# Moving the mixers' weight loads from the SyncE queue to the GpSimd queue

## The chip, the cores and the metric

The kernel runs on one core of one Trainium2 chip. The metric is the device time of one execution in microseconds (us); 1770.11 us is the median of three runs of the kernel before. Engines are named as in the profile: PE is TensorE (matmuls), PEld its weight loads, DVE VectorE, ACT ScalarE, POOL GpSimd, SP SyncE. SP computes nothing; it issues DMAs one after the other, each after its own waits.

## What is computed

Two layers over 256 latent and 256 context tokens of width 1024. Each layer has a mixer (three kinds of attention side by side, gated and merged) and a channel mixer (a dense SwiGLU in layer 0, a top-2 mixture of eight SwiGLU experts in layer 1). Cut to the mixer, which the change is about:

```python
h = modulate(rms_norm(x, norm_mix[i]), sh1, sc1)            # sh1, sc1, g1 ... from c @ w_ada[i]
p_kv, p_q, p_gate = split_last(h @ w_in[i], ...)
y_na  = neighbourhood_attention(q_na, k_na, v_na, k_na_c, v_na_c, rpb[i], n_rows)   # 4 heads
y_gqa = blocked_attention(q_g, k_g, v_g, k_g_c, v_g_c, GQA_SCALE)                   # 8 heads, 2 kv heads
y_mla = blocked_attention(q_m, k_m, v_m, k_m_c, v_m_c, MLA_SCALE)                   # 4 heads
x = x + g1 * merge_branches(y_na, y_gqa, y_mla, p_gate, w_o_na, w_o_gqa, w_o_mla, w_out)
# in layer 0 the context stream goes through the same mixer
```

## The kernel before

All weights are float32 in HBM and are used as pairs of float16 (a high and a low part). A weight tile of up to 128 x 2048 floats (1 MB) is loaded by `load_raw` (L302) into one of four buffers called raw. `split_w` then makes the pair: ACT writes wh (L269), DVE writes wl (L266, from raw and wh). Three such pairs exist (WB = 3). PE multiplies with them (L332 to L334: wh by the high part, wh by the low part, wl by the high part). A raw buffer is free again when the wl of its tile is written; a pair is free when PE has used it. `load_raw` also fetches the adaLN weights of layer 0 (in_ada): those raw tiles are read by PE itself (L426, `ada0_sums`), two tiles for each of twelve sums, four sums in `start` and eight among the jobs of the mixer of layer 0. `load_raw` issues every one of these transfers on SP.

The stages follow one another: `start` (norm, the first four adaLN sums, the first two weight tiles ckv_kg and kna; it has eight further raw buffers), the mixer of layer 0 (about 45 to 440 us), `ffn` (to about 790 us), the mixer of layer 1 (to about 1045 us), then routing and the experts (in_wm, the rest).

In a mixer, PE computes scores of a pair of heads (L936), ACT and DVE make the softmax (L913, L269 and L266 into pn, three buffers), and SP issues a DMA transpose of each pn into pt (L920, three buffers, 4 in a unit of work, 96 in all); PE multiplies pt by the values (L952). `weave` puts the units among the dense work of the mixer. What a buffer's next user must wait for is put in by the framework, and a planner in it lays out each engine's order when the program is built; the order is not simply that of the text. SP's order holds weight loads, loads of the position bias (`head_bias`, L743), rope tables (L386) and the transposes, each behind the one before it. POOL has seven memsets in the whole program, one of them in each mixer (krp, L756).

The functions that name the queue of a load:

Of the kernel before, what the change touches and what calls it, by code (L numbers as in the profile page):

```python
# [249 lines left out]
def trunk(tc, A, out):  # L250
    nc = tc.nc
# [3 lines left out]
    def nm(p="t"):  # L255
        cnt[0] += 1
        return f"{p}{cnt[0]}"
# [10 lines left out]
    def split(hi, lo, src, scale):  # L268
        h = S.activation(hi, src, AF.Copy, scale=scale)  # L269
        return h, stt(lo, src, scale, hi, OP.mult, OP.subtract)  # L270
# [10 lines left out]
    def dram(name, off, w):  # L281
        src = A[name]
        return bass.AP(tensor=src.tensor, offset=src.offset + off, ap=[[w, 128], [1, w]])
# [14 lines left out]
    def new_raw():  # L298
        pool, tag, n = take("raw", raw_slots)
        return pool.tile([128, 2048], FT, tag=tag, bufs=n, name=nm("raw"))  # L300

    def load_raw(name, off, w=2048):  # L302
        raw = new_raw()
        nc.sync.dma_start(raw[:, :w], dram(name, off, w))
        return raw

    def load_w(name, off, w=2048):
        return split_w(load_raw(name, off, w), w)

    def new_parts():  # L310
        pool, tag, n = take("wb", wb_slots)
        return [pool.tile([128, 2048], F16, tag=tag + h, bufs=n, name=nm("w" + h)) for h in "hl"]
# [9 lines left out]
    def split_w(raw, w, parts=None, step=1024):  # L322
        if parts is None:
            parts = new_parts()
        hi, lo = parts
        for a in range(0, w, step):
            b = min(w, a + step)
            issued[0] = split(hi[:, a:b], lo[:, a:b], raw[:, a:b], WS)
        return hi, lo
# [58 lines left out]
    def ada_tile(pool, cb, t):  # L388

        raw = load_raw("ada1", t * 128 * 2048)  # L390
        for j in range(2):
            ch = 2 * t + j
            for s in range(2):
                if s == 1 and ch >= 16:
                    continue
                scr = pool.tile([128, D], F16, tag="scr", bufs=1, name=nm("scr"))
                stt(scr, raw[:, j * D:(j + 1) * D], 0.5, cb[:, s, :], OP.mult, OP.mult,
                    accum_out=mod[1][:, ch, s:s + 1])

    def ada_group(i, g):  # L400

        s = slice(8 * g, 8 * g + 8)
        b = cv(f"b{i}")[:, s]
        n = 1 if (i == 1 and g >= 2) else 2
        m = mod[i][:, s, :n]
        if i == 1:
            add(m, m, b[:, :, None].to_broadcast([128, 8, n]))
        half, what = divmod(g, 3)
        if what == 0:
            V.tensor_scalar(sm[:, i, half, :, :n], m, AS, None, op0=OP.mult)  # L410
        elif what == 1:
            nrm = cv(("nm" if half == 0 else "nf") + str(i))
            u = am[:, i, half, :, :n]
            V.tensor_scalar(u, m, 1.0, AS, op0=OP.add, op1=OP.mult)
            mul(u, u, nrm[:, :, None].to_broadcast([128, 8, n]))
        else:
            V.tensor_scalar(m, m, US, None, op0=OP.mult)

    def ada0_sums(c):


        ps = pg()
        for s in range(2):
            w = load_raw("ada0", (2 * c + s) * 128 * 2048)
            for k in range(4):
                T.matmul(ps[32 * k:32 * k + 32], c32[:, 4 * s + k, :], w[:, 512 * k:512 * k + 512],  # L426
                         start=(s == 0), stop=(s == 1))
        row = st.tile([128, 512], FT, tag="sq", bufs=3, name=nm("row"))
        S.copy(row, ps)
        return row  # L430

    def ada0_cols(row, ch):

        pm = pb([128, 4, 2])
        for k in range(4):
            T.matmul(pm[:, k], row[:, 128 * k:128 * k + 128], cm("pick"), start=True, stop=True)
        m = mod[0][:, ch:ch + 4, :]
        add(m, pm, cv("b0")[:, ch:ch + 4, None].to_broadcast([128, 4, 2]))
        return m
# [12 lines left out]
    def ada0_jobs():  # L452
        q = []
        for c in range(4, 12):
            q.append(lambda c=c: ada0_cols(ada0_sums(c), 4 * c))
            if c % 2:
                q.append(lambda g=c // 2: ada_group(0, g))
        return q

    def ada1_jobs(pool):  # L460
        cb = pool.tile([128, 2, D], FT, name="cb")
        cbf = cb.rearrange("p a b -> p (a b)")

        def prep():
            nc.sync.dma_start(cbf, bass.AP(tensor=A["cc"].tensor, offset=A["cc"].offset, ap=[[0, 128], [1, 2 * D]]))
            t = new_raw()
            S.activation(t, cbf, AF.Tanh, scale=0.5)
            stt(cbf, t, 1.0, cbf, OP.add, OP.mult)

        q = [prep]  # L470
        for t in range(24):
            q.append(lambda t=t: ada_tile(pool, cb, t))
            if t % 4 == 3:
                q.append(lambda g=t // 4: ada_group(1, g))
        return q
# [102 lines left out]
    def start(pool, nrm):  # L578

        raw_slots.append((pool, "raw2", 8))  # L580
        offs, _ = offsets(stream_names(0))
        nrm.alloc()
        for k in range(KD):
            nrm.square(0, k)
        wa = load_w("ws0", offs["ckv_kg"])
        nrm.sums(0)
        first_mod(0)
        wb = load_w("ws0", offs["kna"])
        nrm.spread(0)
        nrm.apply(0, range(0, 4))  # L590
        p4 = [pa() for _ in range(4)]
        jobs = [(p4[0], wa, 0, ALL), (p4[1], wa, 1, ALL), (p4[2], wb, 0, ALL), (p4[3], wb, 1, ALL)]
        first_mod(1)
        group(nrm, jobs, range(0, 4))
        nrm.apply(0, range(4, 8))
        group(nrm, jobs, range(4, 8))
        raw_slots.pop()
        return p4

    def mixer(pool, i, ada_q, nrm, nxt, first=None):  # L600
# [13 lines left out]
        def W(name, n=0):  # L614
            r = load_w(f"ws{i}", offs[name], tile_width(name))
            ada(n)
            return r
# [423 lines left out]
        for j in range(2):  # L1041
            w = W(f"wout{j}")
            for a in range(2):
                out_chunk(w, 2 * j + a, qs)
        w = [W("wout2"), W("wout3")]
        if last:
            presplit.append(split_w(load_raw("wm", 0), 2048, step=2048))
        for p, c in enumerate(halves):
            for d in range(4, 8):
# [64 lines left out]
    with tc.tile_pool(name="s0", bufs=1, reuse_waits="tile") as pool:  # L1114
        p4_0 = start(pool, n_m0)
    with tc.tile_pool(name="m0", bufs=1, reuse_waits="tile") as pool:
        mixer(pool, 0, ada0_jobs(), n_m0, n_f0, p4_0)
    with tc.tile_pool(name="f0", bufs=1, reuse_waits="tile") as pool:
        ffn(pool, ada1_jobs(pool), n_f0, n_m1)
    px = tc.alloc_tile_pool(name="px", bufs=1, reuse_waits="tile")  # L1120
# [8 lines left out]
    ones16 = px.tile([128, 128], F16, name="ones16")  # L1129
    V.memset(ones16, 1.0)  # L1130
    with tc.tile_pool(name="m1", bufs=1, reuse_waits="tile") as pool:
        mixer(pool, 1, [], n_m1, n_f1)


# [322 lines left out]
```

## Time and profile before

| | before |
|---|---|
| time, median of 3 runs (range) | 1770.11 us (1768.71 to 1772.60) |
| the profiled execution, its time | 1770.29 us |
| its span, first to last instruction | 1768.3 us |
| PE, DVE, ACT, POOL busy | 93%, 76%, 59%, 0% |
| granted TensorE clock, mean | 0.976 |
| DMA transposes, weight loads in mixers and start | 96; 68 of in_ws and 24 of in_ada |

The profiled execution lies 0.18 us above the median of the runs, and 2.0 us of its time lie outside its span. The stages differ in their limit, so the views are read stage by stage: the table of stretches gives the busy time of each engine in a window, the waits say what ended the idle time before an instruction, the timeline lists instructions in order of time, and the DMA issues give the time from the issue of a transfer to its landing.

### The profile page before, as it was taken

Reading aid. Unit: us, or ns where it says so; the run is one execution under the profiler, and the core shown is the slowest. Engines: PE = TensorE matmul, PEld = TensorE weight load, DVE = VectorE, ACT = ScalarE, POOL = GpSimd, SP = SyncE. Lnnn points to the kernel's source line nnn. Section 1 sums busy time; section 2 is a strip of 40 time slices with the busy share of each in tenths; the row PEclk is TensorE's granted clock in tenths of the full one; section 3 lists DMA queues with packets and bytes.
Section 4 is the critical chain, followed back from the end, with each engine's and each line's share of the span. In section 5 each row is a group of like instructions: output and inputs, shape, how many; then the busy total and the mean of one; then the engine's idle time right before and its main releaser. Section 6 shows DMA issues by size and latency. Waiting matters only on the chain. (4 is left out here: it accounts for less than half of the span.)

```text
span 1768.3 us, 37807 instructions
## 1 busy us (share of the span) xinstructions
PE 1644.8 (93%) x16157; PEld 1085.5 (61%) x16157; DVE 1351.6 (76%) x1908; ACT 1038.1 (59%) x1354; POOL 1.3 (0%) x7
## 2 busy tenths in 40 slices
PE   5999899999999999999878998999999989999996
PEld 2554335446644444467656877787868686868683
DVE  4577657455886554547787778999999999999996
ACT  3456546343422332224666558888877888878784
POOL 0000000000000000000000000000000000000000
PEclk9999899999999999999998998999999999999998
DMA  9263388452465445534536687999999999999990
GB/s 390 102 155 93 104 257 220 135 193 96 143 219 209 167 161 172 192 111 138 161 79 145 185 306 315 424 413 423 420 415 385 422 418 420 422 400 400 403 384 26
DMA packets 149920, 451.93 MB, mean 256 GB/s; under 512 B 92144, under 2 KB 95344, under 8 KB 103024
## 3 DMA queue, kind: packets, MB, share of 16 engines
q1 hardware_dynamic: 148768, 448.50, 69.0%
q8 instruction: 128, 2.10, 0.5%
q10 hardware_dynamic: 976, 0.94, 0.2%
q14 instruction: 48, 0.39, 0.1%
HBM read 427.38 MB, written 1.05 MB: 242 GB/s over the span
## 5 line engine op out<-in xcount | busy, mean ns | idle before, releaser
L266 DVE SCALAR_TENSOR_TENSOR wl<-raw,wh 128x2048 f16<-128x2048 f32 (+1 forms) x476 | 818.3, 1739 | 54.0 <-ACT wh L269 50.5
L269 ACT ACTIVATE wh<-raw 128x2048 f16<-128x2048 f32 (+1 forms) x474 | 684.3, 1464 | 269.8 <-PE pa L333 94.0
L334 PEld LDWEIGHTS <-wl 128*128 128x128 f16 x4346 | 427.2, 98 | 175.1 <-DVE wl L266 53.3
L332 PEld LDWEIGHTS <-wh 128*128 128x128 f16 x4346 | 428.6, 99 | 129.0 <-issue 17.7
L333 PEld LDWEIGHTS <-wh 128*128 128x128 f16 x4346 | 427.7, 98 | 115.2 <-issue 7.9
L334 PE MATMUL pa<-xg,wl 128*128 128x96 f16 x2816 | 374.6, 207 | 36.2 <-DVE wl L266 35.6
L333 PE MATMUL pa<-xg,wh 128*128 128x96 f16 x2816 | 373.5, 206 | 0.2 <-ACT xg L1254 0.2
L332 PE MATMUL pa<-xg,wh 128*128 128x96 f16 x2816 | 373.4, 206 | 0.0
L332 PE MATMUL pg<-hh,wh 128*128 128x512 f16 (+1 forms) x512 | 170.2, 333 | 5.0 <-ACT gt L972 2.1
L332 PE MATMUL pa<-hh,wh 128*128 128x512 f16 (+1 forms) x480 | 167.5, 355 | 6.1 <-ACT hh L552 6.1
L333 PE MATMUL pa<-hl,wh 128*128 128x512 f16 (+1 forms) x480 | 169.2, 354 | 1.7 <-DVE hl L266 1.7
L334 PE MATMUL pg<-hh,wl 128*128 128x512 f16 (+1 forms) x512 | 169.6, 332 | 0.7 <-DVE wl L266 0.7
L333 PE MATMUL pg<-hl,wh 128*128 128x512 f16 (+1 forms) x512 | 170.0, 332 | 0.0
L334 PE MATMUL pa<-hh,wl 128*128 128x512 f16 (+1 forms) x480 | 169.1, 353 | 0.0
L266 DVE SCALAR_TENSOR_TENSOR scr<-raw,cb 128x1024 f16<-128x1024 f32 x64 | 78.4, 1225 | 78.9 <-DMA raw<-in_ada 77.8
L1317 PE MATMUL pg<-wl,hdh 128*96 128x512 f16 x352 | 133.4, 379 | 0.5 <-DVE wl L266 0.2
L1318 PE MATMUL pg<-wh,hdl 128*96 128x512 f16 x352 | 133.4, 379 | 0.0
L1316 PE MATMUL pg<-wh,hdh 128*96 128x512 f16 x352 | 132.3, 379 | 0.0
L266 DVE SCALAR_TENSOR_TENSOR pn<-P,sml,pn 128x512 f16<-128x512 f32 (+1 forms) x96 | 60.9, 660 | 32.7 <-ACT pn L269 32.2
L269 ACT ACTIVATE pn<-P,sml 128x512 f16<-128x512 f32 (+1 forms) x96 | 59.1, 648 | 38.3 <-DMA pt<-pn 33.3
L913 ACT ACTIVATE P<-pa,sml 128x512 f32<-128x512 f32 (+1 forms) x96 | 58.0, 611 | 32.3 <-DVE sml L911 22.8
L333 PE MATMUL pg<-dl,wh 128*128 128x512 f16 (+1 forms) x198 | 70.4, 355 | 0.0
(250 smaller groups left out, 1860.6 us busy)
## 6 DMA issues: line engine op xcount, KB each, us to landing
raw<-in_wm SPq DMA_DIRECT2D x264, 1024.0 KB, 8.2
raw<-in_ws SPq DMA_DIRECT2D x52, 1024.0 KB, 4.8
raw<-in_ada SPq DMA_DIRECT2D x48, 1024.0 KB, 5.1
raw<-in_ws SPq DMA_DIRECT2D x18, 768.0 KB, 4.9
raw<-in_ws SPq DMA_DIRECT2D x16, 704.0 KB, 4.1
raw<-in_ws SPq DMA_DIRECT2D x16, 640.0 KB, 4.0
raw<-in_ws SPq DMA_DIRECT2D x4, 832.0 KB, 11.6
xT<-in_xt SPq DMA_DIRECT2D x4, 512.0 KB, 6.3
```

Source lines behind the costliest of these rows:

```text
L266: return V.scalar_tensor_tensor(o, a, s, b, op0=op0, op1=op1, **kw)
L269: h = S.activation(hi, src, AF.Copy, scale=scale)
L332: T.matmul(ps, sh, mh, start=first, stop=False)
L333: T.matmul(ps, sh, ml, start=False, stop=False)
L334: T.matmul(ps, sl, mh, start=False, stop=last)
L913: S.activation(P[t], ps[t], AF.Exp, bias=nb[:, t:t + 1], scale=sc, accum_out=sums[:, t:t + 1])
L1316: T.matmul(py, hdh[:, f], w[0][:, c], start=begin, stop=False)
L1317: T.matmul(py, hdh[:, f], w[1][:, c], start=False, stop=False)
L1318: T.matmul(py, hdl[:, f], w[0][:, c], start=False, stop=end)
```

## The change

`load_raw` issues on `queue[0]` instead of on `nc.sync`. This is `nc.gpsimd` while the two mixers are traced and `nc.sync` elsewhere; inside the last mixer it goes back to `nc.sync` just before the first load of the experts' weights. So 82 loads go to POOL: 32 of in_ws and 16 of in_ada in layer 0, where `start` keeps its two and eight on SP, and 34 of in_ws in layer 1. The loads of the bias and the rope tables and the transposes stay on SP. Number and size of the buffers, and all computing, stay.

```diff
+    queue = [nc.sync]
+
     def load_raw(name, off, w=2048):
         raw = new_raw()
-        nc.sync.dma_start(raw[:, :w], dram(name, off, w))
+        queue[0].dma_start(raw[:, :w], dram(name, off, w))
         return raw
...
         if last:
+            queue[0] = nc.sync
             presplit.append(split_w(load_raw("wm", 0), 2048, step=2048))
...
+        queue[0] = nc.gpsimd
         mixer(pool, 0, ada0_jobs(), n_m0, n_f0, p4_0)
+        queue[0] = nc.sync
...
+        queue[0] = nc.gpsimd
         mixer(pool, 1, [], n_m1, n_f1)
```

## Rows read from the trace of the kernel before

**Rows 1.** The page: busy time of the engines; all DMA packets by size.

```profile
PE 1644.8 (93%) x16157; PEld 1085.5 (61%) x16157; DVE 1351.6 (76%) x1908; ACT 1038.1 (59%) x1354; POOL 1.3 (0%) x7
...
DMA packets 149920, 451.93 MB, mean 256 GB/s; under 512 B 92144, under 2 KB 95344, under 8 KB 103024
```

**Rows 2.** Stretches: us; PE, PEld, DVE, ACT, POOL busy; clock; DMA share, GB/s.

```profile
100.00:212.00 112.00, 102.87 (x606) 51.02 (x606) 85.70 (x214) 69.77 (x157) 0.00 (x0) 0.94 0.40 99
212.00:260.00 48.00, 43.64 (x299) 20.33 (x295) 24.97 (x58) 22.58 (x50) 0.00 (x0) 1.00 0.84 267
260.00:345.00 85.00, 84.98 (x487) 40.69 (x480) 51.94 (x102) 42.46 (x87) 0.00 (x0) 1.00 0.67 180
...
900.00:960.00 60.00, 45.55 (x328) 29.80 (x328) 49.67 (x106) 37.59 (x81) 0.00 (x0) 0.86 0.57 132
```

**Rows 3.** Waits, whole span: who waited for whom; us in total, times, longest.

```profile
ACT pn L269 <- DMA pt<-pn: 33.3, 20, 5.5
...
PE pa L936 <- ACT P L913: 8.8, 5, 2.8
PE pb L952 <- DMA pt<-pn: 8.5, 6, 2.7
```

**Rows 4.** Tile pt, 212 to 300 us: transposes' issue (ns) and landing, min/median/max.

```profile
L920 SPq DMA_TRANSPOSE pt<-pn x22: 1194/1238/3943, 220.1 to 289.4; - x22
...
DMA to landing us min/median/max: 2.3/3.9/6.8
```

**Rows 5.** Tile pt, 857 to 987 us: landing of the 32 transposes.

```profile
DMA to landing us min/median/max: 3.1/3.4/4.9
```

**Rows 6.** Timeline from 209 us: start, duration, engine, line, what, count, idle before.

```profile
211.27 2.76 PE L426 MATMUL pg<-raw,c 128*32 128x512 f32 x18
...
212.40 0.34 SPq L304 DMA_DIRECT2D raw<-in_ws  x1
...
214.95 1.92 PE L426 MATMUL pg<-raw,c 128*32 128x512 f32 x14
...
217.40 2.01 ACT L269 ACTIVATE wh<-raw 128x1024 f16<-128x1024 f32 x2
...
220.07 2.51 SPq L920 DMA_TRANSPOSE pt<-pn  x2
...
222.28 0.39 PE L334 MATMUL pg<-hh,wl 128*128 128x512 f16 x1 [0.72 <-DVE wl L266]
...
222.63 1.05 SPq L304 DMA_DIRECT2D raw<-in_ada  x2
```

**Rows 7.** DMA issues, 212.35 to 212.90 us: KB, us to landing.

```profile
raw<-in_ws SPq DMA_DIRECT2D x1, 1024.0 KB, 4.9
```

**Rows 8.** Timeline of SP, start of the program.

```profile
8.50 6.46 SPq L304 DMA_DIRECT2D raw<-in_ada  x4
...
20.83 53.52 SPq L304 DMA_DIRECT2D raw<-in_ws  x8
```

**Rows 9.** DMA issues at 8.50 us (first of four) and at 14.62 us (last).

```profile
raw<-in_ada SPq DMA_DIRECT2D x1, 1024.0 KB, 18.3
...
raw<-in_ada SPq DMA_DIRECT2D x1, 1024.0 KB, 19.6
```

**Rows 10.** Timeline of PE: its use of the first and of the last of these four.

```profile
30.90 1.94 PE L426 MATMUL pg<-raw,c 128*32 128x512 f32 x8
...
42.33 1.06 PE L426 MATMUL pg<-raw,c 128*32 128x512 f32 x8
```

**Rows 11.** Timeline of ACT, layer 0's third branch: it waits for a weight tile.

```profile
360.44 1.36 ACT L269 ACTIVATE wh<-raw 128x1024 f16<-128x1024 f32 x2 [2.20 <-DMA raw<-in_ws]
```

**Rows 12.** Timelines of SP and ACT: a late load of layer 1's mixer, its split.

```profile
1019.79 0.33 SPq L304 DMA_DIRECT2D raw<-in_ws  x1
...
1029.84 1.06 ACT L269 ACTIVATE wh<-raw 128x1024 f16<-128x1024 f32 x1 [0.21 <-PE pg L333]
```

**Rows 13.** Tile krp: POOL's longest instructions, ns min/median/max.

```profile
L756 POOL MEMSET krp<- x2: 417/420/422, 1.0 to 382.7; 128x384 f32 x2
```

## Prediction

> **What bounds the kernel now.** I read the page first: PE is busy for 93% of the span, POOL for nothing [rows 1]. The change touches the start and the two mixers alone, so the table of stretches is next. From 260 to 345 us PE is busy for 84.98 of 85 us [rows 2]: nothing on a queue can be won there. It has 9.1 us of idle time from 100 to 212 us, 4.4 from 212 to 260 and 14.5 from 900 to 960 (112 - 102.87, 48 - 43.64, 60 - 45.55) [rows 2]. These 28 us hold nearly all that a better queue could give back, and 900 to 960 has a granted clock of 0.86, so a little more than the idle time hangs on them. The waits say what ended such idle time: PE waited for transposed probabilities (pt) for 8.5 us in six places, and for ACT's exponential for 8.8 us in five; ACT in turn waited 33.3 us, in 20 places, for a transpose to finish reading a pn buffer [rows 3]. None of the three lines names a weight load. So a queue change can win by quicker transposes, hardly by earlier weights.
>
> **What the change removes.** 82 loads leave SP, at 0.34 us of issue each [rows 6], 28 us of SP time; SP bounds nothing, so this counts only where a load and a transpose hold each other up.
>
> *Loads held behind transposes.* At 216.87 us (214.95 + 1.92) PE has read a raw tile of in_ada, which frees its buffer; the next load into the freed buffers is issued at 222.63, because SP stood at the transposes of 220.07, themselves waiting [rows 6]. So loads here come some 6 us late, and on POOL they would not. Worth to the end: about 0, because from 260 us on PE is full [rows 2] and no wait of [rows 3] is for a raw tile. In layer 1 the load of 1019.79 has some 5 us to spare: landed 4.9 us later [rows 7], 1024.7, it is split at 1029.84 when PE frees the pair [rows 12].
>
> *Transposes held behind loads.* The issue of a transpose takes 1238 ns at the median and up to 3943 where loads fill the queue (212 to 300 us), and it lands after 2.3 to 6.8 us [rows 4]; in layer 1 after 3.1 to 4.9, median 3.4 [rows 5]. If the median came down to the minimum, that were 1.6 us (3.9 - 2.3) for 22 transposes and 0.3 us for 32. But the bytes of the loads are still moved, beside the transposes instead of ahead of them. Ends: -8.5 us (every wait of PE for pt goes) and +7 (below). I take -0.5, near nothing: the landing of 3.1 us in layer 1 is the best of 32, so even alone in the queue a transpose leaves PE most of its wait.
>
> [...]
>
> **What the change adds.** *POOL's own price.* No row shows a DMA issued by POOL. Nearest below: SP's load issue, 0.34 us [rows 6], and POOL's longest instruction, 0.42 us [rows 13]; nearest above: an issue of SP that writes many descriptors, 1.24 us at the median, 3.94 at worst [rows 4]. Against the 0.34 us of now a load so lands between 0.3 us earlier (a queue without others ahead; no row excludes it) and 3.6 us later (3.94 - 0.34). I take 0.9 later (1.24 - 0.34), the ordinary issue that writes many descriptors. [...]
>
> Where does later hurt? Where the buffer, not the queue, held the load, and the use follows at once. The load of 212.40 follows the reading of the tile in its buffer at once (L426 from 211.27), lands 4.9 us later at 217.30, ACT splits it at 217.40, and PE sits 0.72 us at 222.28 until wl is there [rows 6, 7]. This one is on the path: +0.9 us (ends -0.3, +3.6). The tile that ACT awaited 2.20 us at 360.44 [rows 11] is like it on ACT, but PE, full through 345 us and fed from three pairs, has work ahead of it: 0, with +1.8 (twice 0.9) if that cover is gone. In layer 1 the 5 us to spare cover all.
>
> *What queues behind POOL's waits.* A POOL load waits for its raw buffer; behind it stand only later loads, which need later buffers, and the krp memset (0.42 us [rows 13]), awaited long after. Cost 0.
>
> *The start.* Here one queue has an order that is worth something. SP has issued four loads of in_ada from 8.50 to 14.62 us when the mixer's first loads come at 20.83 [rows 8]; these four land 18.3 and 19.6 us after their issue, at 26.8 and 34.2, one each 2.47 us, so the DMA engines have a backlog of 13 us at 20.83 [rows 9]. Now the mixer's first four loads (1 + 0.81 + 0.81 + 1 MB) queue behind it. On POOL they run beside it: 3.62 x 2.47 = 8.9 us of transfers. PE reads the first in_ada tile at 30.90, 4.1 us after it landed, and the last at 42.33, 8.1 us after [rows 9, 10]. With equal shares from 21.2 (20.83 + 0.34) the first lands at 21.2 + 2 x 5.6 = 32.4, 1.5 us after PE wants it, and the last at 34.2 + 8.9 = 43.1, 0.8 after. PE runs its instructions in their order and is full afterwards, so this stays: +1.5 us. Ends: 0 (the older backlog goes first, as now) and +4.8 (the new loads go first, 8.9 - 4.1).
>
> **Sum.** +1.5 (start) + 0.9 (load of 212.40) - 0.5 (transposes) + 0 = +1.9 us on the profiled execution's 1770.29 (1768.3 of span and 2.0 outside it): 1772.2, and as the median of the runs is 0.18 lower, 1772.0 us, 0.1% above before. A measurement of this kernel tells about 0.2% (3.5 us) from no change, so faster means below 1766.6 and slower above 1773.7. The single ends add up to 1770.1 + 0 - 0.3 - 8.5 = 1761.3 and, without the +7 that is a rival's, 1770.1 + 4.8 + 3.6 + 1.8 = 1780.3.
>
> The planner lays out the engines' orders anew, with loads it no longer has to fit between transposes. What that moves, no row tells; the idle time it can fill is the 28 us above. I count it in the chances.
>
> **Rivals.**
> 1. *Faster: the transposes decide.* With short issues always, ACT's waits for pn shorten, and PE's 8.5 us for pt and the part of the 8.8 us behind ACT go. For it: the issues of 3.94 us [rows 4], PE's 14.5 idle us beside transposes [rows 2, 3]. Against: from 100 to 212 us loads are few (99 GB/s) and PE is idle for 9.1 us all the same [rows 2]. With all 8.5 and nothing lost, 1770.1 - 8.5 = 1761.6; with the start's 1.5 lost, 1763.
> 2. *Slower: POOL is slow to write a load's descriptors.* If a load lands 3.6 us later, the one at 212.40 costs 3.6 and, where the cover at 360 us is thinner than I think, two further ones 1.8 together, and the start 1.5 to 4.8: 1770.1 + 3.6 + 1.8 + 3 = 1778.5. It decides from some 1.5 us of extra time on. For it: the backlog and the lack of slack in [rows 6, 9, 11]; against: layer 1, with 5 us to spare. [...]
> 3. *Slower: packets alternate.* A transpose is some 960 packets (92144 under 512 B for 96), a load 128 [rows 1]. If the engines take turns between queues packet by packet, every transpose beside a load waits out that load, 2.5 us, also one issued after it. ACT's 11 waits in the two stretches with loads would grow by 27 us, of which PE, at 8.5 for 33.3 [rows 3], sees 7: 1779.
> 4. *Nothing happens,* because loads wait for buffers and not for the queue, as in layer 1: 1770. It lies within the forecast's own case.
>
> **Chances.** Forecast with rival 4, 42%: its own range 1768 to 1775, 36 points within 0.2%, 6 slower. Rival 1, 22%: 20 faster, 2 same. Rival 2, 24%: 22 slower, 2 same. Rival 3, 12%: 10 slower, 2 same. So faster 0.20, same 0.42, slower 0.38. The range of 8 in 10 takes in most of rivals 1 to 3: 1761 to 1781.
>
> **What would show it.** In the trace of the changed kernel: SP holds transposes, bias and rope alone in the mixers, and the issue of a transpose no longer exceeds 2 us from 212 to 300 us. PE's readings of in_ada tiles at the start come 1 to 2 us later and the first PE idle time there names a DMA. The load of g0_3 (the one of 212.40) lands some 6 us after its buffer is free, not 5. The transposes of layer 1 still land after 3 us or more, and PE from 900 to 960 us is still idle for some 14 us. Wrong, if that idle time falls by 5 us or more (rival 1), if raw tiles appear among the waits of ACT and PE in the mixers with more than a few us (rival 2), or if transposes land after 6 us and more beside loads (rival 3).

## The result and the profile after

The changed kernel takes 1798.03 us (median of 4 runs, 1797.66 to 1801.09) beside 1770.42 of the kernel before on the same chip: ratio 1.0155, 95% interval 1.014 to 1.017. It is 27.6 us slower; the prediction was 1772.0 with a range of 1761 to 1781. The profiled execution of after took 1801.09 us, the longest of the four; its span is 1799.2.

The page of after: busy time of the engines, and the new queue of POOL (packets, MB, share of the 16 DMA engines). [Rows 1] has the same line of before.

```profile
PE 1652.8 (92%) x16157; PEld 1089.2 (61%) x16157; DVE 1350.9 (75%) x1908; ACT 1038.5 (58%) x1354; POOL 44.8 (2%) x89
...
q0 software_dynamic: 11808, 74.19, 12.1%
```

PE is busy 8.0 us longer with the same 16157 matmuls, the span is 30.9 us longer: 22.9 us are new idle time of PE, 8.0 are matmuls at a lower clock (0.967 granted on the mean, 0.976 in before). To see where, I cut both traces at the same pieces of work: from the first transpose to the FFN's first activation (mixer of layer 0), to the first transpose of layer 1 (FFN), and to the first load of in_wm (mixer of layer 1). Stretches of before (start:end, length, PE, PEld, DVE, ACT, POOL busy, clock, DMA share, GB/s):

```profile
95.20:471.90 376.70, 359.49 (x2175) 188.23 (x2174) 238.69 (x517) 182.35 (x370) 0.42 (x1) 0.97 0.53 155
471.90:857.90 386.00, 381.97 (x2020) 197.09 (x2018) 232.61 (x390) 125.81 (x190) 0.00 (x0) 1.00 0.48 167
857.90:1026.80 168.90, 146.03 (x1206) 112.64 (x1205) 134.01 (x293) 102.80 (x208) 0.00 (x0) 0.92 0.62 156
```

The same three of after:

```profile
95.90:497.10 401.20, 364.50 (x2175) 190.26 (x2174) 238.19 (x517) 182.17 (x370) 20.08 (x38) 0.95 0.51 146
497.10:882.50 385.40, 381.75 (x2020) 197.13 (x2018) 232.56 (x390) 126.00 (x190) 6.78 (x13) 1.00 0.48 167
882.50:1057.70 175.20, 148.68 (x1205) 114.30 (x1204) 133.58 (x293) 102.93 (x208) 11.64 (x22) 0.88 0.59 150
```

Layer 0's mixer is 24.5 us longer (401.2 - 376.7): 19.5 of idle time (36.7 against 17.2) and 5.0 of slower matmuls. Layer 1's is 6.3 us longer, 3.6 and 2.7. The start is 0.7 longer, the FFN 0.6 shorter, the experts unchanged (741.5 in both). Of the three waits shown in [rows 3] the first and the last grew, and one that was 1.6 us in before (longest 0.7) now stands behind them with 22.2 (waits of after: who for whom, us, times, longest):

```profile
ACT pn L269 <- DMA pt<-pn: 41.6, 20, 5.1
...
PE pb L954 <- DMA pt<-pn: 24.4, 8, 10.3
...
ACT qg L269 <- PE pb L954: 22.2, 7, 9.9
```

PE's wait for transposes went from 8.5 to 24.4 us, the longest one from 2.7 to 10.3. The transposes from 212 to 300 us, to be held beside [rows 4] (issue in ns, then landing in us, min/median/max each):

```profile
L922 SPq DMA_TRANSPOSE pt<-pn x22: 1188/1264/2128, 211.4 to 299.2; - x22
...
DMA to landing us min/median/max: 2.3/2.8/17.0
```

The longest issue became short, as the change would have it (2128 ns, not 3943; the median stayed, 1264 against 1238), and the median landing fell from 3.9 to 2.8 us; but the worst rose from 6.8 to 17.0. Behind two late transposes PE sits idle for 16.7 us (10.30 + 6.41), most of the 19.5 of layer 0. The timeline around the first (start, duration, engine, what, idle before):

```profile
238.58 2.58 SPq L922 DMA_TRANSPOSE pt<-pn  x2
...
239.98 0.53 POOL L306 DMA_DIRECT2D raw<-in_ws  x1 [9.87 <-PE pg L428]
...
240.84 0.53 POOL L306 DMA_DIRECT2D raw<-in_ada  x1 [0.33 <-PE pg L428]
...
243.64 0.53 POOL L306 DMA_DIRECT2D raw<-in_ada  x1 [2.27 <-PE pg L428]
...
244.50 0.53 POOL L306 DMA_DIRECT2D raw<-in_ada  x1 [0.33 <-PE pg L428]
...
256.88 0.64 PE L954 MATMUL pb<-pt,vh 128*64 128x256 f16 x3 [10.30 <-DMA pt<-pn]
```

The DMA issues of 239.9 to 240.1 us (KB each, us to landing):

```profile
raw<-in_ws POOLq DMA_DIRECT2D x1, 1024.0 KB, 5.8
pt<-pn SPq DMA_TRANSPOSE x1, 17.0
```

The second of the two transposes has just been issued when PE frees four raw buffers one after the other, and POOL starts a load into each. The loads, issued after the transpose, take turns with it, and it lands 17.0 us after its issue, a fifth load having been started at 250.46; PE sits 10.30 us. On SP these loads stood behind the transposes. At 278.6 us the same happens again (a transpose lands after 12.1 us, PE sits 6.41). While they share the engines here, the two queues get nearly the same number of packets. DMA queues of after, 250 to 253 us (q0 is POOL's, q1 SP's):

```profile
q0 software_dynamic: 153, 1.15, 91.6%
q1 hardware_dynamic: 151, 0.04, 7.0%
```

153 packets, all but 13 of them of 8 KB, against 151 of 256 B: the transposes' queue moves 0.04 MB while the loads' moves 1.15. Counts as close as these agree with turns, one packet of each queue at a time.

From within each of the two waits on PE has half its clock (granted 0.50), where before it had 1.00 from 212 to 345 us [rows 2]:

```profile
248.80:262.40 13.60, 5.52 (x30) 2.59 (x30) 1.43 (x3) 1.37 (x6) 0.53 (x1) 0.50 0.73 264
286.30:296.60 10.30, 5.90 (x31) 3.16 (x32) 1.78 (x7) 2.60 (x8) 0.00 (x0) 0.50 0.49 144
```

### The profile page after: what moved, and what is told of

It is laid out like the page before. It is cut to its first block, busy times and chain, and to the rows that moved or that the text cites. A ratio compares the mean times of both kernels' runs of the same rounds, so it can differ in the third digit from the quotient of the medians.

```text
span 1799.2 us, 37870 instructions
## 1 busy us (share of the span) xinstructions
PE 1652.8 (92%) x16157; PEld 1089.2 (61%) x16157; DVE 1350.9 (75%) x1908; ACT 1038.5 (58%) x1354; POOL 44.8 (2%) x89
## 3 DMA queue, kind: packets, MB, share of 16 engines
q0 software_dynamic: 11808, 74.19, 12.1%
## 5 line engine op out<-in xcount | busy, mean ns | idle before, releaser
L334 PE MATMUL pg<-hh,wh 128*128 128x512 f16 (+1 forms) x512 | 171.0, 334 | 6.3 <-ACT gt L974 2.5
L336 PE MATMUL pg<-dh,wl 128*128 128x512 f16 (+1 forms) x198 | 70.4, 355 | 0.0
```

Of the source, the lines that this page charges most:

```text
L334: T.matmul(ps, sh, mh, start=first, stop=False)
L336: T.matmul(ps, sl, mh, start=False, stop=last)
```

## The experiments

Theory 1: DMA engines give every queue a turn, packet by packet; a transpose of SP's queue waits out loads that another queue starts while it is under way. Theory 2: the price is POOL's own (its issue, and whatever is particular to the queue that the page calls software_dynamic). Theory 3: the planner, with the loads off SP, laid out PE's order anew, and this order costs the time. All three can give 1798, so the runs move the queue, the order and the meetings one at a time. The first 95 us of a profiled execution can differ by 5 us with nothing changed in them (95.2 us to the first transpose in before, 100.1 in the run with POOL in layer 1 alone), so beside the times stands the length of layer 0's mixer, cut as above (376.7 in before), and PE's idle time in it (17.2), each from the one profiled execution of its run.

| run | median us (runs) | ratio to before, 95% | layer 0's mixer, PE idle in it | worst landing of a transpose |
|---|---|---|---|---|
| before | 1769.2 to 1771.6 | 1 | 376.7, 17.2 | 6.8 |
| after | 1798.0 (4) | 1.014 to 1.017 | 401.2, 36.7 | 17.0 |
| layer0_only | 1793.1 (4) | 1.011 to 1.015 | 399.0, 36.4 | 16.3 |
| layer1_only | 1778.6 (5) | 1.003 to 1.007 | 377.4, 17.5 | 7.1 |
| ws_on_sp | 1776.6 (10) | 1.002 to 1.005 | 380.2, 21.6 | 7.4 |
| ada_on_sp | 1792.1 (4) | 1.009 to 1.015 | 392.5, 32.4 | 17.0 |
| quarter_packets | 1812.4 (4) | 1.020 to 1.027 | 411.6, 44.0 | 16.4 |
| one_in_flight | 1816.1 (4) | 1.021 to 1.029 | 400.7, 30.5 | 7.8 |
| pool_old_order | 1797.3 (4) | 1.010 to 1.017 | 399.1, 32.7 | 17.3 |
| sp_new_order | 1780.5 (4) | 1.003 to 1.007 | 384.8, 25.2 | 5.6 |
| pool_after_transposes | 1791.1 (4) | 1.009 to 1.013 | 391.9, 22.7 | 7.8 |
| one_wait | 1791.2 (4) | 1.010 to 1.014 | 393.1, 27.5 | 11.0 |
| two_waits | 1787.2 (4) | 1.006 to 1.013 | 389.2, 28.2 | 8.8 |

**Transposes and loads by themselves.** The kernel does one group of DMAs after another, as

```
for q in (sp, act, pool):
    phase(0, 1, q, True)
    phase(0, 4, q, True)
    phase(1, 4, q, False)
    phase(1, 4, q, True)
```

(so many transposes on SP, so many 1 MB loads on q, the loads first or not)

> The whole computation is left out: only transposes of 128x1024 f16 on SP and 1 MB loads, in small groups one after another. Theory 1 (DMA engines take turns between queues, packet by packet): a transpose alone lands in about 2.3 us; issued just before four loads of another engine's queue it lands after 10 us or more, and as late beside loads of ACT's queue as of POOL's; ahead of four loads in SP's own queue it lands as alone; with one load of POOL beside it about 5 us, with two about 7. Theory 2 (something of POOL's alone, its descriptors being written in software): slow beside POOL's loads, under 4 us beside ACT's; a single POOL load alone lands 1 us or more later than one of SP. Theory 3 (the new order of the instructions, not the queues, made the time): under 4 us beside loads of any queue.

Measured, first of two rounds. Rows of five windows, DMA issues (KB, us to landing) and, where two queues share the engines, their packets: a transpose alone; one issued ahead of four loads in SP's queue; one behind four loads in SP's queue; one issued just before four loads of ACT; one issued just after the first of four loads of POOL:

```profile
pt<-pn SPq DMA_TRANSPOSE x1, 3.1
...
raw<-in_ws SPq DMA_DIRECT2D x4, 1024.0 KB, 8.2
pt<-pn SPq DMA_TRANSPOSE x1, 3.1
...
pt<-pn SPq DMA_TRANSPOSE x1, 11.6
...
q10 hardware_dynamic: 576, 4.19, 78.5%
q1 hardware_dynamic: 1056, 0.26, 8.4%
raw<-in_ws ACTq DMA_DIRECT2D x4, 1024.0 KB, 8.8
pt<-pn SPq DMA_TRANSPOSE x1, 13.8
...
q0 software_dynamic: 576, 4.19, 77.6%
q1 hardware_dynamic: 1056, 0.26, 10.2%
raw<-in_ws POOLq DMA_DIRECT2D x4, 1024.0 KB, 8.2
pt<-pn SPq DMA_TRANSPOSE x1, 13.3
```

Ahead of four loads in the same queue a transpose is as quick as alone (3.1); beside four loads of another queue it takes 13.8 us with ACT's (12.5 when it is issued after the second load) and 13.3 with POOL's (8.8 when it is issued before them). So it is not POOL: theory 2 falls for the landing, and theory 3 too. The size follows from the packets: a transpose is here 1024 packets of 256 B, 64 for each of 16 engines if they are spread evenly, a load 128 of 8 KB, 8 for each (144 are counted, with 16 small ones; 1056 with 32). With 64 turns to take, by this estimate, a transpose is only half through when four loads have had all of theirs, so it waits out every load that comes: 4 x 2.5 us, the 2.47 of the prediction, and its own 3.1 are 13.1, an estimate. The second round gave 14.4 and 12.6 us with ACT's loads and 9.1 and 17.6 with POOL's; the last is 4.5 us more than turns account for.

The price of POOL's path is small. A single load of SP, then of POOL, alone:

```profile
raw<-in_ws SPq DMA_DIRECT2D x1, 1024.0 KB, 4.8
...
raw<-in_ws POOLq DMA_DIRECT2D x1, 1024.0 KB, 5.1
```

A miss of theory 1: beside a single load of POOL it gave 5 us, and both landed after more than 8:

```profile
raw<-in_ws POOLq DMA_DIRECT2D x1, 1024.0 KB, 8.2
pt<-pn SPq DMA_TRANSPOSE x1, 8.3
```

Beside two loads of POOL the transpose took 9.7 us, beside one in the next bare kernel 6.2 and 10.9. From 171.0 to 173.5 us of the meeting shown the two queues together moved only 110 GB/s, so sharing can slow them beyond the turns; why was not tried.

**Half of the change.** The line `queue[0] = nc.gpsimd` is taken out of one mixer, or one kind of load goes back to SP:

```diff
-        queue[0].dma_start(raw[:, :w], dram(name, off, w))
+        (nc.sync if name == "ada0" else queue[0]).dma_start(raw[:, :w], dram(name, off, w))
```

> Loads on POOL in the mixer of layer 0 alone. Theory 1 (transposes wait out bursts of loads): the bursts of in_ada loads are in this mixer, so nearly all of the loss stays, some 25 us, about 1795. Theory 2 (a price on every POOL load): the loss goes by the number of loads, 60 of 82, some 20 us, about 1790. Theory 3 (new order): not fixed; anything from 1770 to 1798.

> Loads on POOL in the mixer of layer 1 alone. Theory 1: no in_ada loads here, single loads beside transposes: some 6 us, about 1776. Theory 2: 22 of 82 loads, some 8 us, about 1778. Theory 3: anything from 1770 to 1798.

> The change without its in_ada loads: those 16 stay on SP, the 66 weight loads of the mixers are on POOL. The planner's order of the engines is here almost that of the change (137 of 36284 rows of PE differ). Theory 1 (a transpose gives a turn to every packet of another queue, so bursts in another queue cost): the bursts around 240 us are mostly in_ada and go, the weight loads beside transposes stay: 8 us of layer 1 and some 5 to 10 of the 22 in layer 0, about 1785. Theory 2 (a price for each load of POOL): 66 of 82, about 1793. Theory 3 (the new order): about 1798.

> The other half: the 16 in_ada loads on POOL, the weight loads on SP. The planner's order of the engines is almost that of the kernel before (123 of 36284 rows of PE differ). Theory 1: bursts of in_ada beside transposes in layer 0 stay, layer 1 is as before: 10 to 17 us above before, about 1784. Theory 2: 16 of 82 loads, about 1776. Theory 3: about 1771.

Layer 0 alone costs 22 us, layer 1 alone 7, together 29 for the 28 of the change: the places add up. Of the kinds, the weight loads alone cost 22 us and the in_ada loads alone 6. This is nearer to theories 2 and 3 (1793 and 1776; 1798 and 1771) than to theory 1 as I had put it (1785 and 1784). The trace of ada_on_sp shows why: the burst of in_ada loads at 240 us is gone, but at 259.7 three weight loads start behind a transpose of 259.40, it lands after 17.0 us and PE sits 13.9 us. With the in_ada loads on POOL, transposes and bursts miss each other (none over 7.4 us). But this trace is of an execution of 1770.16 us, one of two near the time of before, while the other eight took 1775 to 1780; what those lost it does not show. The two traces show that the kind of load alone does not decide: which loads meet a transpose changes with the schedule. Theory 3 had not fallen by these two, since the order of ada_on_sp is nearly that of the change and that of ws_on_sp nearly that of before.

Turns do not account for all of it. Three loads of 768 KB would add 3 x 1.9 us to the transpose's own 3.1, some 9 us by the same estimate, not 17.0. In that meeting the engines move little: DMA queues of ada_on_sp from 264 to 270 us, 93% busy with 0.33 MB, 55 GB/s, against 267 GB/s at 0.84 in before from 212 to 260 us [rows 2]. The counts are not equal here.

```profile
q0 software_dynamic: 52, 0.31, 70.0%
q1 hardware_dynamic: 89, 0.02, 23.3%
```

**Smaller loads, one load at a time.**

```diff
-        queue[0].dma_start(raw[:, :w], dram(name, off, w))
+        whole, step = dram(name, off, w), 512 if queue[0] is nc.gpsimd else w
+        for a in range(0, w, step):
+            b = min(w, a + step)
+            queue[0].dma_start(raw[:, a:b], whole[:, a:b])
```

> The changed kernel with each mixer load cut into loads of 512 columns, so packets of 2 KB in place of 8 KB: same bytes, same queue, four times the issues on POOL. Theory 1 (turns by packet): a transpose's packets each wait for a quarter as much, so transposes beside a burst land in 5 to 8 us instead of 12 to 17, and 12 to 25 of the 28 us come back: 1773 to 1786. Theory 2 (POOL's price per load): four times as many issues, so clearly slower than 1798. Theory 3 (new order): about 1798 as long as the order is that of the change.

It took 1812 us, and the worst landings stayed (16.4). By its time that is what theory 2 asked for; by the landings it is theory 1 with a wrong size of mine: the packets shrank to 4 KB, not 2 (22816 on POOL's queue for the 74.2 MB that took 11808), so the same bytes take twice the turns beside a transpose. The next kernel, bare groups with rows of 8 KB, 2 KB and 512 B, shows the turns once more.

> The whole computation is left out: 1 MB loads of POOL and of SP whose rows in memory are 8 KB, 2 KB or 512 B long, with and without a transpose of 128x1024 f16 beside them. Theory 1 (turns by packet): with 8 KB rows the transpose lands after 9 to 18 us beside four loads of POOL; with shorter packets, so many turns at less each: at 2 KB 6 to 10 us, at 512 B 4 to 6; four loads alone take longer the shorter their packets. Theory 2 (POOL): the same landing for all three or worse with short rows, whose descriptors are more. Turns by bytes would leave the landing the same for all three.

Four loads of POOL with 2 KB rows and a transpose, six microseconds of both under way:

```profile
q0 software_dynamic: 545, 2.12, 91.7%
q1 hardware_dynamic: 549, 0.14, 10.6%
```

545 packets against 549: turn for turn again. A POOL load with 2 KB or 512 B rows is moved in packets of 4 KB (2.12 MB in 545; with 512 B rows 0.81 MB in 205), so my run could not go below that; the transpose landed after 13.2, 13.8 and 12.5 us behind the first of four loads with rows of 8 KB, 2 KB and 512 B. Equal landings are what turns by bytes would give too, but 0.14 MB against 2.12 rules these out. So shorter rows are no remedy for a transpose that finds a load under way. One issued just ahead of the four loads, as the late ones of the changed kernel were ahead of most of theirs, landed after 11.2, 6.0 and 3.1 us (9.7, 6.6 and 3.1 in the second round): there 512 B rows did keep it as quick as alone, while the last of four such loads by themselves landed after 14.3 us instead of 11.1. No kernel run had 512 B rows.

```diff
+            with behind(*arrived):
                 queue[0].dma_start(raw[:, :w], dram(name, off, w))
+            arrived[:] = [G.tensor_copy(seen, raw[:, 0:1])]
```

> The changed kernel with a small POOL copy out of each loaded tile ahead of the next load, so that POOL has one load under way at a time; order of the loads unchanged. Theory 1: a transpose can meet the 8 packets per engine of one load, or two in turn, so none beside loads lands after more than 8 to 10 us, PE's waits for pt fall by half, and 10 to 20 of the 28 us come back, 1778 to 1788, less what loads that now come late cost (four loads in a row take 22 us in place of 11). Theory 2 (price per load): no gain, 1798 or more. Theory 3: not fixed.

The landings did what theory 1 said (none over 7.8, PE's wait for pt 11.5 us, not 24.4), the time did not: 1816. Now the loads come late; ACT waits 21.9 us for weight tiles, 3.9 in before and 6.3 in after:

```profile
ACT wh L269 <- DMA raw<-in_ws: 21.9, 10, 4.1
```

So this run does not tell how much of the loss the meetings are.

**Order against queue.** All 7967 instructions of PE, DVE and ACT up to the end of the second mixer are tied into one order per engine: the loads on POOL in the order of before, and the loads on SP in the order of after. `want` is that order; the tie sets the order of issue alone and adds no wait.

```diff
+        for a, b in zip(want, want[1:]):
+            tc.add_manual_dep(b, a.name, mybir.DependencyInfo(
+                mybir.DependencyClass.NoSync, mybir.DependencyReason.DATA), reason="in_order")
```

> Mixer loads on POOL as in the change, but PE, DVE and ACT held, up to the end of the second mixer, to exactly the order that they have in the kernel before. Theory 1 (transposes give a turn to each packet of the loads of another queue, and PE waits for them): the order is not the cause, so 15 to 30 us above before remain, 1785 to 1800, with single transposes landing after 10 us and more. Theory 2 (price per POOL load): about the same, 1790 to 1800, but with transposes that land within 7 us and loads that come late. Theory 3 (the new order is what costs): as before, 1770, give or take 4.

> All loads on SP as in the kernel before, but PE, DVE and ACT held, up to the end of the second mixer, to exactly the order that they have in the changed kernel. Theory 1: transposes and loads keep out of each other's way in one queue, so no transpose lands after more than 7 to 8 us, and the time is that of before, 1767 to 1777. Theory 2: the same, about 1770. Theory 3: the loss comes with the order, 1790 to 1798.

POOL with the old order takes 1797.3, as the change; SP with the new order 1780.5. Waits of the first, and its longest; then the same wait of the second:

```profile
PE pb L1037 <- DMA pt<-pn: 24.1, 8, 10.6
...
257.31 0.64 PE L1037 MATMUL pb<-pt,vh 128*64 128x256 f16 x3 [10.63 <-DMA pt<-pn]
```

```profile
PE pb L1037 <- DMA pt<-pn: 10.0, 10, 3.3
```

The queue brings the loss and the late transposes with it (17.3 us); theory 3 falls as the cause. It had a point: the new order, tied, costs 9 us by itself, more than theory 1 allowed. What the tie alone costs was not tried; the FFN takes 387.1 to 387.4 us in the runs with it, against 386.0 in before and 385.4 in the change. The two do not add up (26 + 9 against 27.6), so how much of the changed kernel's time the order carries, between 1.8 (27.6 - 25.8) and 9 us, stays open.

**Taking the meetings away.** To the kernel with POOL and the old order a copy of one element per partition on POOL is added, out of a transposed tile, ahead of the next load; the loads stay on POOL.

```diff
                 nc.sync.dma_start_transpose(pt[:, t, :nk // 64], pn.rearrange("p a b -> p (a b)"))
+                gates.append(G.tensor_copy(seen, pt[:, t, 0, 0:1]).ins)
```

First behind every transpose, then behind the 40th alone (the one that landed after 17.3 us), then behind the 40th and the 48th.

> Mixer loads on POOL, PE, DVE and ACT in the order of the kernel before (as in the run with the old order), and on POOL a small copy out of each transposed tile, placed among the loads as the transposes stand among them on SP in the kernel before: a POOL load that stood behind a transpose on SP now waits until that transpose has landed. Theory 1 (loads started on top of a transpose under way make it late): the landings of 10 us and more go, none over 8, and most of the 26 us come back, 1771 to 1783; not all, because a load also waits for the landing and so comes some 3 us later than on SP. Theory 2 (the price is POOL's issuing or descriptors): POOL issues the same loads and more work beside, so 1795 or more.

> As the run with POOL loads and the old order, but for a single small copy on POOL, out of the tile of the 40th transpose, ahead of the next load: the transpose that landed 17.3 us after its issue at 239.96 us there now lands before the four loads behind it start, 3 us later than there. Theory 1 (loads started on top of a transpose under way make it late): that transpose lands in some 3 us, the idle time of PE of 10.6 us behind it goes, and with it the stretch at half the clock that follows (10.3 us, half of it lost), so 10 to 16 us come back: 1782 to 1788. Theory 2 (POOL's issuing or descriptors): 1797, unchanged; the loads are as many.

> The run with one wait, and a second of the same kind: the three weight loads that in it met the transposes of 263.83 to 270.61 us wait until the 48th transpose has landed. Theory 1: the idle time of 6.6 us behind the transpose that landed after 11 us goes, and with it the 17 us at half the clock that follow, so 10 to 15 us more come back, 1775 to 1782, unless the loads meet yet other transposes further on. Theory 2: 1791 to 1797, unchanged.

One wait: the 40th transpose lands after 3.2 us, and the 10.63 us are gone. But three weight loads now start at 265.7 to 267.4, a transpose of 267.38 lands after 11.0 us, and PE waits there and runs at half its clock behind it. Landing of the 39th and 40th transposes; PE's wait at the new meeting; the stretch behind it:

```profile
DMA to landing us min/median/max: 3.2/3.2/3.2
...
274.51 0.39 PE L1044 MATMUL pb<-pt,vh 128*64 128x256 f16 x1 [6.57 <-DMA pt<-pn]
...
272.10:289.10 17.00, 14.59 (x65) 8.29 (x66) 5.62 (x15) 5.31 (x15) 0.53 (x1) 0.50 0.59 197
```

Layer 0's mixer goes from 399.1 to 393.1 us with one wait and to 389.2 with two, the time from 1797.3 to 1791.2 and 1787.2: each meeting taken away gives back 4 to 6 us, less than expected (10 to 16, then 10 to 15); after the first the loads meet others later. The intervals of the times overlap, and beside each run's own before the two steps give back 8 us (25.8, 20.5 and 18.1 above it). It is layer 0's mixer, with the start left out, that shows them: it is 9.9 us shorter, and PE's wait for pt in it fell from 15.7 to 5.1 us. Theory 2, which gave no change at all, fits neither the landings nor this mixer. With a wait behind every transpose none lands after more than 7.8 us and PE's wait for pt is that of before (8.2 against 8.5 us), yet the time is 1791.1. What is left of layer 0's mixer there, 15.2 us, is 5.5 of idle time (22.7 against 17.2) and 9.7 of slower matmuls: PE was granted half its clock in two stretches in which before had all of it.

```profile
PE pb L1049 <- DMA pt<-pn: 8.2, 8, 2.4
```

```profile
240.80:254.50 13.70, 12.57 (x69) 6.68 (x70) 2.04 (x8) 2.17 (x6) 2.58 (x7) 0.50 0.74 248
275.00:288.60 13.60, 13.34 (x62) 7.89 (x62) 5.95 (x14) 4.54 (x13) 2.60 (x6) 0.50 0.64 203
```

Ahead of them PE sat 2.00 us at 238.2 (for ACT) and 2.36 at 272.9 (for a transpose). Before, too, sat 2.00 us at 256.9 and kept its clock, so what decided there stays open. Shown is: the queue causes the loss, and transposes that wait beside loads of another queue are a part of it; two such places give back 8 to 10 of 26 us. Not shown is how the other 16 to 18 divide among small meetings (with one and two waits the median landing in layer 1 is 4.2 and 3.9 us, against 3.4 in before), loads that come later, and the clock. No kernel run had its loads on ACT's queue: that a price of POOL's own has no share in the rest, while the computing runs that the bare groups leave out, is not shown either. No kernel was faster than before.

## Why the prediction was wrong

- **The failing step is the term of the transposes**, -0.5 with +7 as a rival. The sentence "the bytes of the loads are still moved, beside the transposes instead of ahead of them" was right and pointed to the loss; I then took a value near nothing by looking at medians. The median landing did fall [rows 4], from 3.9 to 2.8 us. The cost came from the maximum, 17.0: PE's wait for transposes, which the term let fall by 0.5 us, rose by 15.9 (8.5 to 24.4). The range left the +7 out as a rival's; with it the ends would have reached 1787, and the measured 1798 still lies above.
- **Rival 3 named the mechanism, its size was off.** "If the engines take turns between queues packet by packet, every transpose beside a load waits out that load, 2.5 us, also one issued after it": the counts show such turns (153 packets to 151, 545 to 549), but for the slowest meeting (52 to 89), and a transpose issued just before four loads of ACT landed after 13.8 us. But I counted one load for a transpose. PE frees four buffers within 5 us, four loads start, and a transpose with 64 turns to take waits out all of them: 13 us in the first round of the bare groups, 17 in the kernel, where a fifth load came in. Then I spread the delay over ACT's waits and gave PE 8.5 of every 33.3 us [rows 3]; a wait of 17 us is beyond any cover, and PE saw 10.3 of it. Nor did the price hold the clock: 8.0 us of the 30.9.
- **"From 260 to 345 us nothing on a queue can be won there"** [rows 2] holds, but a full stretch can lose: PE's busy time in the same window fell from 84.98 to 78.07 us of 85, part of it at the lower clock. I had asked only what idle time could be given back. After:

```profile
260.00:345.00 85.00, 78.07 (x430) 36.29 (x430) 53.20 (x114) 41.34 (x90) 5.82 (x11) 0.93 0.59 152
```

- **A second queue gained nothing:** no kernel with loads on POOL was faster than before, and beside the loads the queue with the smaller packets lost: a transpose lands after 3.1 us alone, after 8.8 to 17.6 beside four loads of another queue with rows of 8 KB.
- **The start**, +1.5: the last in_ada load, issued at 14.63, landed at 43.0, as equal shares gave it (43.1 worked out), the first already at 28.3 (32.4 worked out); first and last of the four, to be held beside [rows 9]:

```profile
raw<-in_ada SPq DMA_DIRECT2D x1, 1024.0 KB, 19.8
...
raw<-in_ada SPq DMA_DIRECT2D x1, 1024.0 KB, 28.4
```

  PE waited 1.3 us for them, 1.0 in before, and the first transpose came only 0.7 us later than before: the term was too large.
- **The load of g0_3**, +0.9: it landed 5.7 us after its issue and some 6.0 after its buffer was free, close to the 5.8 worked out, against 4.9 [rows 7]. It cost nothing; PE's idle time at that place is what it was in [rows 6]:

```profile
228.21 0.39 PE L336 MATMUL pg<-hh,wl 128*128 128x512 f16 x1 [0.72 <-DVE wl L266]
```

  From the start of ACT's split to this matmul went 3.9 us (224.35 to 228.21), 4.9 before [rows 6]: there was 1 us of cover that I had not seen.
- **What was right:** raw tiles hardly appear among the waits in the mixers (ACT waits 6.3 us for those of in_ws, 3.9 before), so rival 2 was rightly no forecast, and POOL's price per load is small (0.3 us of landing, 0.53 us of issue for 0.33). The +0.9 was my estimate from the issue of a transpose, 1.24 us [rows 4]; that it is long because it writes many descriptors, and that POOL would be as long over a load's, no run shows. **Not foreseen in size:** the planner's new order, which I left to the chances: 9 us by itself, with the tie. The sign that I had named for rival 3, landings of 6 us and more beside loads, is the one that came.

## What to carry to other kernels

Before a load is moved off a queue, ask what its place in that queue protects. Here a transpose, a DMA of many small packets, landed after 3.1 us ahead of four loads in its own queue, as alone, while in another queue the loads took turns with it, also those that started after it, and it landed after 8.8 to 17.6 us. Price such a meeting by the loads that one release of buffers starts together (four here, and a fifth while the transpose was still under way), and by the worst landing (17.0 us, from 6.8), not the median (2.8, from 3.9). Of the wait, what is longer than the cover counts (10.3 us of the 17.0), and so does a lower clock (8.0 us of slower matmuls here). The full stretch from 260 to 345 us had nothing to win, but it lost 6.9 us of busy time (84.98 to 78.07).

## What the runs showed of the hardware

- Two queues shared the DMA engines turn for turn in packets at two sizes: 153 to 151 (8 KB against 256 B, after), 545 to 549 (4 KB against 256 B, bare groups). In the slowest meeting the counts were 52 to 89 (loads of weights alone on POOL).
- Sharing could cost more than one after the other: a transpose and one load, 3.1 and 5.1 us alone, landed together after 6.2 to 10.9 us (the transpose, in the two bare kernels) and 5.4 to 10.8 (the load); in the slowest meeting the engines were 93% busy with 55 GB/s. Why was not tried.
- POOL's loads of 2 KB or 512 B rows were moved in packets of 4 KB (2.12 MB in 545, 0.81 MB in 205); a 1 MB load of POOL alone landed 0.3 us later than one of SP (5.1 against 4.8).
- PE's clock was halved (granted 0.50) for 10 to 17 us behind waits of 6 to 10 us, and in one run behind waits of 2.0 and 2.4 us; in before a wait of 2.0 us left it at 1.00.
